# A 512-byte-piece fill of the last output rows on ScalarE's DMA queue at the start, and one store left whole, in an L1 row normalisation

## The chip, the cores and the metric

The kernel runs on one core of one Trainium2 chip. The metric is the device time of one execution in microseconds (us). Three executions of the kernel before took 317.07, 317.03 and 316.71 us, a median of 317.03 us.

## The reference, cut to what matters

The input is 32 x 512 x 1024 numbers in float32, that is 16384 rows of 1024. Each row is divided by the sum of its absolute values:

```python
sums = np.sum(np.abs(x), axis=-1, keepdims=True)
return (x / (sums + 1e-8)).astype(np.float32)
```

67.11 MB are read and 67.11 MB are written.

## The kernel before, in words

The 16384 rows are cut into eleven pieces. A piece covers all 128 partitions of the on-chip memory, with 12 rows of 4 KB per partition (6.29 MB); the last piece (number 10, `last` in the code) has 8 rows per partition (4.19 MB). Pieces 0, 1 and 10 come out of the first 4096 rows, where each partition has 32 consecutive rows: rows 0 to 11 are piece 0, rows 12 to 23 are piece 1, rows 24 to 31 are piece 10. Pieces 2 to 9 follow one after the other. There are four buffers of one piece each.

Every piece goes through the same four steps.

- **Load** (L86): one DMA issued by SyncE (SP). The argument `max_dma_last_dim` sets how large a contiguous run one DMA piece may carry: 48 KB (the whole run of a partition) for loads 0 and 1, 24 KB for the others. A DMA over 128 partitions is spread over the 16 DMA engines, 8 partitions on each, so each engine gets 8 pieces of 48 KB for load 0, 8 of 48 KB for load 1, and 16 of 24 KB for each load from 2 to 9 (load 10: 16 of 16 KB).
- **Sum** (L47): VectorE (DVE) sums the absolute values of each row, then adds epsilon (L54) and takes the reciprocal (L56).
- **Scale**: most rows are multiplied on VectorE in one instruction (L58); for pieces 0, 1, 2, 9 and 10 the table `split` gives some rows to ScalarE (ACT, L68) and some to single-row instructions on VectorE (L65).
- **Store** (L91): DMAs issued by ScalarE's queue, with 24 KB runs for pieces 0 to 8 and the whole run for pieces 9 and 10. Stores 7 and 8 (`last - 3` and `last - 2`) are issued as two DMAs of half a piece each, all others as one.

The order of the program is written out by hand (`manual_schedule`): loads 0 to 3 first, then for each piece its compute, its store, and the load of the piece four further on, which takes over the buffer and so waits until that store has landed. Loads are on SP's queue, stores on ScalarE's queue; both queues are served by the same 16 DMA engines. The waits between engines and DMAs are put in by the framework. It gives every DMA one of eight completion semaphores in turn, and a DMA also waits for the one that held its semaphore before.

Of the kernel before, what the change touches and what calls it, by code (L numbers as in the profile page):

```python
# [1 line left out]

# [4 lines left out]

FP32 = mybir.dt.float32
EPS = 1e-8


@with_exitstack
def kernel(
    ctx: ExitStack,
    tc: tile.TileContext,
    x: bass.AP,
    out: bass.AP,
):
    nc = tc.nc
    P = nc.NUM_PARTITIONS  # L20

    x_flat = x.flatten_outer_dims()
    out_flat = out.flatten_outer_dims()
    n, d = x_flat.shape

    R = 12
    BUFS = 4
    HEAD = 32
    per_partition = n // P
    assert n % P == 0 and (per_partition - HEAD) % R == 0  # L30
    rows = [R] * ((per_partition - HEAD) // R + 2) + [HEAD - 2 * R]

    def piece(flat, i):
        head = flat[: P * HEAD, :].rearrange("(p r) d -> p r d", p=P)
        if i < 2:
            return head[:, R * i : R * (i + 1), :]
        if i == len(rows) - 1:
            return head[:, 2 * R :, :]
        a = P * (HEAD + R * (i - 2))
        return flat[a : a + P * R, :].rearrange("(p r) d -> p r d", p=P)  # L40

    sbuf = ctx.enter_context(tc.tile_pool(name="sbuf", bufs=BUFS))
    stats = ctx.enter_context(tc.tile_pool(name="stats", bufs=len(rows)))

    def normalize(x_tile, k, kv, kt):
        s = stats.tile([P, R], FP32)
        nc.vector.tensor_reduce(  # L47
            out=s[:, :k],
            in_=x_tile[:, :k, :],
            axis=mybir.AxisListType.X,  # L50
            op=mybir.AluOpType.add,
            apply_absolute_value=True,
        )
        nc.vector.tensor_scalar_add(out=s[:, :k], in0=s[:, :k], scalar1=EPS)  # L54
        inv = stats.tile([P, R], FP32)
        nc.vector.reciprocal(out=inv[:, :k], in_=s[:, :k])  # L56
        if kv:
            nc.vector.tensor_mul(  # L58
                out=x_tile[:, :kv, :],
                in0=x_tile[:, :kv, :],  # L60
                in1=inv[:, :kv].unsqueeze(2).to_broadcast([P, kv, d]),
            )
        for r in range(kv, kv + kt):
            row = x_tile[:, r, :]
            nc.vector.tensor_scalar_mul(out=row, in0=row, scalar1=inv[:, r : r + 1])  # L65
        for r in range(kv + kt, k):
            row = x_tile[:, r, :]
            nc.scalar.activation(  # L68
                out=row,
                in_=row,  # L70
                func=mybir.ActivationFunctionType.Copy,
                scale=inv[:, r : r + 1],
            )

    last = len(rows) - 1
    split = {0: (3, 4), 1: (0, 3), 2: (0, 3), last - 1: (0, 2), last: (5, 3)}

    tiles = {}

    HALF, WHOLE = 24576, 49152

    def load(i):
        x_tile = tiles[i] = sbuf.tile([P, R, d], FP32, name="x_tile")
        nc.sync.dma_start(out=x_tile[:, : rows[i], :], in_=piece(x_flat, i), max_dma_last_dim=WHOLE if i < 2 else HALF)  # L86

    def store(i):
        parts = [(0, R // 2), (R // 2, R)] if i in (last - 3, last - 2) else [(0, rows[i])]
        for a, b in parts:  # L90
            nc.scalar.dma_start(  # L91
                out=piece(out_flat, i)[:, a:b, :],
                in_=tiles[i][:, a:b, :],
                max_dma_last_dim=WHOLE if i >= last - 1 else HALF,
            )

    def compute(i):
        k = rows[i]
        kt, ks = split.get(i, (0, 0))
        normalize(tiles[i], k, k - kt - ks, kt)  # L100

    with tc.manual_schedule():
        for i in range(BUFS):
            load(i)
        for i in range(len(rows)):
            compute(i)
            store(i)
            if i + BUFS < len(rows):
                load(i + BUFS)


# [1 line left out]
_INS = ['x']  # L113
_OUTS = [((32, 512, 1024), 'float32')]


# [23 lines left out]
```

## Time and profile before

| quantity | value |
|---|---|
| median of three executions | 317.03 us |
| the profiled execution | 316.79 us |
| span of its instructions in the profile | 315.2 us |
| VectorE busy | 261.1 us (83%) |
| ScalarE busy | 17.4 us (6%) |
| read from and written to the off-chip memory (HBM) | 67.11 MB each, 426 GB/s over the span |
| first load issued; first sum starts | 0.73 us; 17.72 us |
| store 0 issued | 38.75 us |
| last store issued | 292.51 us |

The profile is of one execution. Its span runs from the first to the last recorded instruction; the device time of the same execution is 1.6 us longer, because of what lies around it. Views of the trace give, for any stretch of the span, the busy time of each engine, the busy share of the 16 DMA engines, the bytes they moved and how many DMA packets each queue had. A packet is booked in the stretch in which it starts, so the rate of a short stretch jumps, and only stretches of many packets can be compared closely. In these views q1 is SP's queue (the loads) and q10 is ScalarE's queue (the stores). The trace also holds every packet's own start, duration, size and queue.

### The profile page before, as it was taken

The numbers are of one execution on the slowest core, as the hardware profiler recorded it, in microseconds if no ns is written. First come the engines' busy times: TensorE is split into PE (matmuls) and PEld (weight loads), VectorE is DVE, ScalarE is ACT, GpSimd is POOL, SyncE is SP. The second block draws the span as 40 slices with busy tenths as digits, with TensorE's granted clock in tenths as the row PEclk, the third lists the DMA queues.
The fourth block names the chain that finished last, engine by engine and source line by source line (L and its number), as shares of the span: only waits on it lengthen the run. The fifth ranks groups of instructions, "written<-read, shape, count | busy, mean of one in ns | idle before, by whom it ended". The sixth has DMA issues, their size and how long they took to land.

```text
span 315.2 us, 169 instructions
## 1 busy us (share of the span) xinstructions
DVE 261.1 (83%) x51; ACT 17.4 (6%) x16; POOL 0.2 (0%) x4
## 2 busy tenths in 40 slices
DVE  0079999999999999979996997999699969999100
ACT  0010403004000000000000000000000000203000
POOL 0000000000000000000000000000000000000000
DMA  7999999999999999999999999999999999999997
GB/s 299 499 399 409 440 399 418 430 449 418 430 449 418 430 449 424 424 449 427 421 449 427 421 449 434 415 449 434 415 449 434 415 433 449 416 433 499 399 403 329
DMA packets 5504, 134.22 MB, mean 426 GB/s; under 512 B 384, under 2 KB 384, under 8 KB 384
## 3 DMA queue, kind: packets, MB, share of 16 engines
q1 hardware_dynamic: 2736, 67.11, 49.9%
q10 hardware_dynamic: 2768, 67.11, 49.4%
HBM read 67.11 MB, written 67.11 MB: 426 GB/s over the span
## 4 chain that ended last, share of the span: by engine, by line
DVE 41%; DMA 33%; another core or an unknown queue 18%; SPq 0%; issue 0%; DVEq 0%
DVE s L47 23%; DMA x_tile<-in_x_dram 17%; DVE x_tile L58 15%; DMA out_dram<-x_tile 15%; DVE x_tile L65 2%; DVE inv L56 0%; DVE s L54 0%; SPq L86 0%; DVEq L135 0%
## 5 line engine op out<-in xcount | busy, mean ns | idle before, releaser
L47 DVE TENSOR_REDUCE s<-x_tile 128x12 f32<-128x12288 f32 (+1 forms) x11 | 138.2, 12561 | 30.0 <-DMA x_tile<-in_x_dram 30.0
L58 DVE TENSOR_TENSOR x_tile<-x_tile,inv 128x12288 f32<-128x12288 f32 (+3 forms) x10 | 113.6, 11358 | 0.5
L68 ACT ACTIVATE x_tile<-x_tile,inv 128x1024 f32<-128x1024 f32 x15 | 16.1, 1138 | 257.1 <-DVE inv L56 257.1
L65 DVE TENSOR_SCALAR x_tile<-x_tile,inv 128x1024 f32<-128x1024 f32 x8 | 5.5, 748 | 0.0
L56 DVE RECIPROCAL inv<-s 128x12 f32<-128x12 f32 (+1 forms) x11 | 2.5, 226 | 0.4
L68 ACT ACT_TABLE_LOAD x1 | 1.3, 1283 | 17.8 <-DMA x_tile<-in_x_dram 17.8
L54 DVE TENSOR_SCALAR s<-s 128x12 f32<-128x12 f32 (+1 forms) x11 | 1.9, 173 | 0.4
L124 POOL MEMSET const-uint8-127<- 128x1 uint8 x1 | 0.1, 102 | 0.0
L124 POOL MEMSET const-bfloat16-1.0<- 128x1 bf16 x1 | 0.1, 101 | 0.0
L124 POOL MEMSET const-float32-0.0<- 128x1 f32 x1 | 0.1, 98 | 0.2 <-issue 0.2
L124 POOL MEMSET const-float32-1.0<- 128x1 f32 x1 | 0.1, 98 | 0.0
## 6 DMA issues: line engine op xcount, KB each, us to landing
x_tile<-in_x_dram SPq DMA_DIRECT2D x10, 6144.0 KB, 37.6
out_dram<-x_tile ACTq DMA_DIRECT2D x8, 6144.0 KB, 47.2
out_dram<-x_tile ACTq DMA_DIRECT2D x4, 3072.0 KB, 36.5
x_tile<-in_x_dram SPq DMA_DIRECT2D x1, 4096.0 KB, 32.0
out_dram<-x_tile ACTq DMA_DIRECT2D x1, 4096.0 KB, 21.7
```

Of the source, the lines that this page charges most:

```text
L47: nc.vector.tensor_reduce(out=s[:, :k], in_=x_tile[:, :k, :], axis=mybir.AxisListType.X, op=mybir.AluOpType.add, apply_absolute_value=True,)
L54: nc.vector.tensor_scalar_add(out=s[:, :k], in0=s[:, :k], scalar1=EPS)
L56: nc.vector.reciprocal(out=inv[:, :k], in_=s[:, :k])
L58: nc.vector.tensor_mul(out=x_tile[:, :kv, :], in0=x_tile[:, :kv, :], in1=inv[:, :kv].unsqueeze(2).to_broadcast([P, kv, d]),)
L65: nc.vector.tensor_scalar_mul(out=row, in0=row, scalar1=inv[:, r : r + 1])
L68: nc.scalar.activation(out=row, in_=row, func=mybir.ActivationFunctionType.Copy, scale=inv[:, r : r + 1],)
L124: nc = _bacc.Bacc("TRN2", target_bir_lowering=False, num_devices=1)
```

## The change

A second pool with one small tile is added. After load 0 is issued, a new function `fill` sets this tile (128 x 128 float32) to zero on VectorE, and ScalarE's queue issues one DMA from it. The DMA writes the first 384 numbers of the first row of piece 10 in every partition, as 3 chunks of 512 bytes: 3 chunks x 8 partitions is 24 pieces of 512 bytes on each DMA engine, 196,608 bytes in all. Store 10, the last one, writes the final values over these bytes. Besides, store 7 (`last - 3`) is no longer split: it is issued as one DMA with 24 KB runs, like stores 0 to 6. Store 8 stays split.

```diff
     sbuf = ctx.enter_context(tc.tile_pool(name="sbuf", bufs=BUFS))
+    once = ctx.enter_context(tc.tile_pool(name="once", bufs=1))
     stats = ctx.enter_context(tc.tile_pool(name="stats", bufs=len(rows)))
...
-        parts = [(0, R // 2), (R // 2, R)] if i in (last - 3, last - 2) else [(0, rows[i])]
+        parts = [(0, R // 2), (R // 2, R)] if i == last - 2 else [(0, rows[i])]
...
+    CHUNKS, WIDTH = 3, 128
+
+    def fill():
+        zeros = once.tile([P, WIDTH], FP32, name="zeros")
+        nc.vector.memset(zeros, 0.0)
+        nc.scalar.dma_start(
+            out=piece(out_flat, last)[:, 0, : CHUNKS * WIDTH].rearrange("p (c w) -> p c w", c=CHUNKS),
+            in_=zeros.unsqueeze(1).to_broadcast([P, CHUNKS, WIDTH]),
+            max_dma_last_dim=4 * WIDTH,
+        )
+
     with tc.manual_schedule():
-        for i in range(BUFS):
+        load(0)
+        fill()
+        for i in range(1, BUFS):
             load(i)
```

## The prediction

> **What bounds the kernel now.** I read the page first.
>
> ```profile
> span 315.2 us, 169 instructions
> ...
> DVE 261.1 (83%) x51; ACT 17.4 (6%) x16; POOL 0.2 (0%) x4
> ...
> DMA  7999999999999999999999999999999999999997
> ...
> DMA packets 5504, 134.22 MB, mean 426 GB/s; under 512 B 384, under 2 KB 384, under 8 KB 384
> ...
> q1 hardware_dynamic: 2736, 67.11, 49.9%
> q10 hardware_dynamic: 2768, 67.11, 49.4%
> ```
>
> No compute engine fills the span, but the DMA row is full from the second slice to the next to last, and the packets of both queues together fill 99.3% of sixteen engines' span. The waits say the same from VectorE's side: it has 30 us of idle time, all of it for loads.
>
> ```profile
> DVE s L47 <- DMA x_tile<-in_x_dram: 30.0, 6, 17.7
> ```
>
> So bytes bound it, and the question is at which moments the DMA engines are not moving them. I cut the span into stretches of 27.25 us, thirty 24 KB pieces each (columns: stretch, length, busy time of DVE, ACT and POOL, clock, DMA share, GB/s).
>
> ```profile
> 13.42:40.67 27.25, 22.84 (x8) 5.55 (x5) 0.00 (x0) 1.00 1.00 431
> 40.67:67.92 27.25, 27.15 (x5) 3.23 (x3) 0.00 (x0) 1.00 1.00 420
> 67.92:95.17 27.25, 27.15 (x5) 3.23 (x3) 0.00 (x0) 1.00 1.00 433
> ...
> 204.17:231.42 27.25, 24.50 (x5) 0.00 (x0) 0.00 (x0) 1.00 1.00 433
> ```
>
> Loads alone (first line) run at 431, loads and stores together at 433. One stretch is short: 420 against 433 is 27.25 x 13 / 433 = 0.82 us lost. It holds the moment when ScalarE's queue gets its first work. Store 0 is issued at 38.75, and the view of the DMA queues from 40.48 to 43.17 shows
>
> ```profile
> DMA packets 33, 0.81 MB, mean 301 GB/s; under 512 B 0, under 2 KB 0, under 8 KB 0
> ...
> q1 hardware_dynamic: 33, 0.81, 100.3%
> ```
>
> that is only load packets, "busy" all the time, but at 301: 2.69 x (1 - 301/433) = 0.82 us again. In the single packet records a 24 KB packet takes 0.912 us wherever it stands, except two per engine here; together these are 0.82 us too long (mean of 16 engines, 0.77 to 0.86 in the six I took apart). Then the first store packet goes at 43.17, 4.4 us after the issue. After this the two queues alternate, one piece of each, to the end, with no gap; all other packets after 43 us are 0.02 us too long in sum. The first packet of load 0 is also too long, 2.62 against 1.815 us, by 0.80 on the mean. So an idle queue that gets work seems to cost each engine about 0.8 us: once at the start for SP's queue, once at 41 us for ScalarE's. I read the second as a fixed cost of waking a queue; that it is this and not, say, the first write to HBM is an inference.
>
> The budget closes: first packet at 1.73, all packets at their usual rate 310.07, the two losses 0.80 + 0.82, the small rest 0.02: 313.44, and the engines' last packets end between 313.33 and 313.85. Then 1.3 us to the span's end, and 1.6 us more to the execution's 316.79. The median of 317.03 is 0.24 above this; I add my sum to the median.
>
> **The change part by part.**
>
> *The fill's bytes.* DMA engines have no slack, so this is paid in full. The usual distance from one packet to the next is 0.607 us for 16 KB, 0.908 for 24 KB, 1.210 for 32 KB, 1.812 for 48 KB, 0.0055 for the 4-byte completion packets. That is 36.8 ps per byte and about 5 ns per packet, so 512 bytes cost 19 + 5 = 24 ns and 24 of them 0.57 us. The trace has no packet between 4 bytes and 16 KB. From below, the bytes alone are 0.45 us; from above, a small write that holds its engine for twice my value gives 1.14. I take 0.57, as 4-byte packets, also small, cost only their 5 ns.
>
> *The stall at 41 us.* If ScalarE's queue never runs dry between the start and store 0, waking it happens at about 2 us. ScalarE waits for VectorE's memset (nearest rows: 0.17 us for a 128x12 operation, 0.75 for 128x1024), so it issues at about 1.1, against 0.73 for load 0. Load 0's first packets start 1.0 us after their issue and lose their 0.80 until about 2.6, so the wake of ScalarE's queue, from about 2.1 on, falls on engines of which most still wait for their first bytes. Between hidden (gain 0.82) and not hidden (gain 0) I take hidden, because both queues' losses have the same size and look like one latency, and two latencies can run together.
>
> *Does the queue stay awake?* One piece of each queue goes in turn, and even the 4-byte completion packets take a turn of their own, so 24 small pieces last as long as 24 load pieces: 8 of load 0, 8 of load 1, 8 of load 2. In the records the 8th piece of load 2 ends at 38.8; with 0.57 us of fill ahead, 39.4. Store 0's issue comes 8 x 24 ns = 0.19 later with load 0's landing, at 38.94, and its first packets can start 1.0 later, at 39.9. So the queue is dry for 0.5 us, or not at all if its pieces go one or two load pieces late (0.9 us each), as store 0's first did. This is close; I take the second.
>
> [...] The records of this trace show turns of one piece, but none of 512 bytes.
>
> [...]
>
> *The memset and the early issue.* VectorE is idle until 17.72 and ScalarE until 17.77, so both are hidden. SP's loads 1 to 3 are issued after the fill in the program's text but on another engine, with no wait on it. Eight small pieces make load 0 land 0.19 us later, and VectorE's first sum with it; VectorE's work ends at 292.5 while stores keep the DMA engines busy to 313.8, so it has some 11 us of cover (store 9 ends at 304.2 and store 10 is issued at 292.5). Without that cover it would cost these 0.19 us.
>
> *New waits.* Load 5 takes the fill's semaphore and waits for it, but is issued past 100 us, some 60 us after the fill has landed. Store 10 must follow the fill too, at 292. Nothing queues behind either.
>
> *Store 7 whole.* Removed: one DMA issue of ScalarE's queue (0.34 to 0.48 us on an engine that is 94% idle) and one 4-byte packet per engine, 0.0055 us, which pays for the fill's own. Moved: its first half no longer lands at 260.1 but with the second, at 272.9. No load follows into this buffer, so nobody waits. Store 9's semaphore is then one last held by load 8, long done. Below and above: nothing.
>
> Sum: -0.82 + 0.57 = **-0.25 us**: 316.54 for the profiled execution, 316.8 on the median.
>
> **The rivals.**
>
> *A. The wake is hidden at the start* (as above): -0.25, or up to +0.2 if half of it shows. For it: the engines stand still at the start anyway. Against: ScalarE's queue wakes some 0.4 us after SP's, so part may stick out. 316.8 (316.5 to 317.3).
>
> *B. The stall moves but does not shrink*, or the change does not do what it says and it stays at 41 us (several small pieces go in one turn, or the cost belongs to something that only a large store meets): +0.57, 317.6; 318.2 with small pieces at 48 ns. For it: nothing in the trace shows two wakes overlapping.
>
> *C. It is paid twice* (this one ends slower): the queue wakes unhidden at 2 us, runs dry before store 0's descriptors come, and wakes again at 41 us: 0.82 + 0.57 = +1.39, 318.4. It decides when the last small piece goes over 0.5 us before 39.9, which is where my reckoning without lag puts it, and when an empty queue loses its state at once.
>
> *D. Stall gone and small pieces nearly free*, because they are written while the engine waits for a load's reads: their 5 ns each are 0.12, so -0.82 + 0.12 = -0.70, 316.3. Against: loads and stores in turn run at 433, no faster than loads alone at 431, so nothing is covered in that way.
>
> **How the numbers follow.** A 0.48, B 0.30, C 0.14, D 0.08. The bound of 0.2%, 0.63 us, is about what a measurement of this kernel can tell from no change. A lies within it. B lies within it at 24 ns a piece and outside from 27 ns; I split it in halves. C is slower; D is just faster. Faster 0.08, same 0.63, slower 0.29. The range: from 316.2 (D) to 318.2 (B with its upper cost), which leaves out C and a little of the others, some 0.18 in all. A's own range is 316.5 to 317.3.
>
> **What would show it.** In the changed profile q10 has 24 x 16 = 384 more packets, "under 2 KB" but not "under 512 B", and 16 fewer and 16 more 4-byte ones. If A holds, the stretch after 40 us is at 433 and q10 packets appear in it at once; the first packets of q1 take about as long as before. B shows the start (306 GB/s between 1.70 and 4.27 us now) slow for longer, or 420 still in that stretch; C both. If small pieces cost more than 24 ns, loads 0 and 1 land later than by 0.2 and 0.4 us. I am wrong altogether if another stretch, above all one after 250 us, falls below 433, or if VectorE's last work moves past 304.

## The result, and the profile after

The changed kernel takes 317.62 us against 316.85 for the kernel before (medians of 12 executions each): a ratio of 1.0027, 95% interval 1.0018 to 1.0035, or +0.77 us (0.57 to 1.11). It is slower, by 0.27%; the forecast was 316.8, faster.

Its page, with the counts of DMA packets, the two queues, and the last line of the list of DMA issues (KB, then us from issue to landing):

```profile
span 315.8 us, 171 instructions
...
DMA packets 5888, 134.42 MB, mean 426 GB/s; under 512 B 384, under 2 KB 768, under 8 KB 768
...
q1 hardware_dynamic: 2736, 67.11, 49.8%
q10 hardware_dynamic: 3152, 67.31, 49.5%
...
out_dram<-zeros ACTq DMA_DIRECT2D x1, 192.0 KB, 39.0
```

The 384 small packets are there (768 under 2 KB, still 384 under 512 bytes), on q10. The fill landed 39.0 us after its issue. The single packet records give the kernel's last packet the end 314.31 (313.85 before). The timeline gives the moments that the prediction reckoned with:

```profile
1.02 0.45 ACTq L108 DMA_DIRECT2D out_dram<-zeros  x1
17.93 12.95 DVE L48 TENSOR_REDUCE s<-x_tile 128x12 f32<-128x12288 f32 x1 [16.94 <-DMA x_tile<-in_x_dram]
...
38.96 0.38 ACTq L92 DMA_DIRECT2D out_dram<-x_tile  x1
```

The first sum starts 0.21 us later than before (0.19 was expected) and store 0 is issued at 38.96 (38.94). So the early part went as reckoned. Now the stretches of 27.25 us (length, busy times, clock, DMA share, GB/s):

```profile
13.42:40.67 27.25, 22.63 (x8) 5.55 (x5) 0.00 (x0) 1.00 1.02 437
40.67:67.92 27.25, 27.15 (x5) 3.23 (x3) 0.00 (x0) 1.00 1.00 418
67.92:95.17 27.25, 27.15 (x5) 3.23 (x3) 0.00 (x0) 1.00 1.00 433
```

The short stretch is still there, 418 where it was 420. The view of the DMA queues from 40.90 to 43.50, which holds two whole turns of every engine:

```profile
DMA packets 32, 0.79 MB, mean 302 GB/s; under 512 B 0, under 2 KB 0, under 8 KB 0
...
q1 hardware_dynamic: 32, 0.79, 102.3%
```

32 load packets of 24 KB, none of q10, at 302 GB/s: the same picture as before, 0.5 us later (the first packet of store 0 starts at 43.65, before at 43.17). By the single packet records the long packets here add up to 0.84 us per engine (0.82 before). At the start, load 0's first packets are too long by 0.70 (0.80 before), but they also start 0.10 later on the mean, so these two cancel. The small pieces are 0.0235 us apart from what follows them, 0.564 us for 24. The engines' last packets end 0.55 us later on the mean of the 16 (313.54 to 314.09): that is the fill's bytes to within 0.02. The span grew by more, 0.68 us; the rest lies behind the last packet and is taken up in the account of the sum below.

So the time came from the fill itself, and the stall that it was to move stayed. The question for the chip is what that stall belongs to. Two theories at first: **Dry**, which the prediction rests on: it is the cost of waking a queue that has run dry; in the changed kernel the last small piece went at 38.3 to 38.8 and the fill's completion packets at 39.3 to 39.7, while store 0, issued at 38.96, had its first piece at 43.65. And **Large store**: it comes with the first large store pieces among loads, whatever the queue did before.

### The profile page after: what moved, and what is told of

Read it like the earlier page. It is cut to its first block, busy times and chain, and to the rows that moved or that the text cites. A ratio compares the mean times of both kernels' runs of the same rounds, so it can differ in the third digit from the quotient of the medians.

```text
span 315.8 us, 171 instructions
## 1 busy us (share of the span) xinstructions
DVE 261.4 (83%) x52; ACT 17.4 (6%) x16; POOL 0.2 (0%) x4
## 4 chain that ended last, share of the span: by engine, by line
DVE 41%; DMA 33%; another core or an unknown queue 18%; SPq 0%; issue 0%; DVEq 0%
DVE s L48 23%; DMA x_tile<-in_x_dram 18%; DVE x_tile L59 15%; DMA out_dram<-x_tile 15%; DVE x_tile L66 1%; DVE inv L57 0%; DVE s L55 0%; SPq L87 0%; DVEq L149 0%
```

## Experiments

In what follows "the loss" is the sum of what load packets take beyond their usual time, per engine, the mean of 16, read from the packet records of the one profiled execution of each kernel.

**fill32: the queue fed until store 0 comes.**

```diff
-    CHUNKS, WIDTH = 3, 128
+    CHUNKS, WIDTH = 4, 128
```

> Four chunks instead of three: 32 pieces of 512 bytes per DMA engine. In the changed kernel the last of the 24 small pieces ended at about 39.4 us and store 0's descriptors came some 0.5 us later. Theory Dry (an engine loses about 0.82 us when ScalarE's queue gets work after it has run dry): the queue is still fed when store 0 comes, the two long load packets at 41 us vanish, and the time is the kernel before - 0.82 + 32 x 0.0235 = -0.07 us, about 316.8. Theory Large store (the loss belongs to the first large piece that the queue carries, whatever went before): the two long packets are still there just before store 0's first piece, and the time is before + 0.75 = 317.6, a little above the changed kernel.

Measured: 317.99 against 316.78 us, ratio 1.0037 (1.0025 to 1.0050), above what either theory had. Store 0 was issued at 39.13, and small pieces went out until 46.8 to 47.2, one after each load piece. Two stretches of the DMA queues, each with three load pieces and three small ones per engine; first 41.5 to 44.3 us:

```profile
DMA packets 96, 1.20 MB, mean 430 GB/s; under 512 B 0, under 2 KB 48, under 8 KB 48
...
q10 hardware_dynamic: 48, 0.02, 2.9%
```

then 44.3 to 47.5 us:

```profile
DMA packets 96, 1.20 MB, mean 376 GB/s; under 512 B 0, under 2 KB 48, under 8 KB 48
...
q10 hardware_dynamic: 48, 0.02, 2.5%
```

The same packets, but 376 for 430 GB/s. The queue is awake, as q10's 48 packets show, and load packets are long all the same (0.49 us by the records). They stand 5 us after store 0's issue, and just ahead of its first piece at 47.8. So this loss stands ahead of the first store piece in the order of packets; it does not follow the issue and does not need a dry queue. Dry falls. Odd in this profile: another 0.46 us of slightly long load packets between 12 and 36 us. The kernel after and the next one don't have them; the two amounts together are about the usual loss.

**fill32_64b: the same with 64-byte pieces.**

```diff
-    CHUNKS, WIDTH = 3, 128
+    CHUNKS, WIDTH = 4, 16
```

> 32 pieces of 64 bytes per DMA engine. By the spacing of packets (36.8 ps per byte and 4.7 ns per packet) a piece costs 7 ns and all of them 0.23 us. Theory Dry: before - 0.82 + 0.23 = -0.59 us, about 316.25, faster than both kernels. Theory Large store: before + 0.23, about 317.1. If pieces under 512 bytes cost as much as those of 512, 0.5 us is to be added to either.

Measured: 317.27 against 316.78, ratio 1.0015 (1.0006 to 1.0024): +0.49 us, interval 0.19 to 0.76. The windows:

```profile
13.42:40.67 27.25, 22.86 (x8) 5.55 (x5) 0.00 (x0) 1.00 1.00 429
40.67:67.92 27.25, 27.15 (x5) 3.23 (x3) 0.00 (x0) 1.00 1.00 420
```

The loss is 0.72 us although small pieces went out until 45.4 to 45.9 and the first store piece followed at 46.9. The 7 ns for a 64-byte piece stay an estimate from the spacing of other packets; by the times, 32 of them came with +0.49 us where fill32's 32 of 512 bytes came with +1.21, so pieces under 512 bytes are not dearer here. Large store (+0.23) is within the interval, Dry (-0.59) is not.

**no_fill: the other half of the change alone.**

```diff
         load(0)
-        fill()
         for i in range(1, BUFS):
```

> Only the second half of the change: store 7 left whole, no zeros written. Both theories: no difference from the kernel before beyond 0.1 us, as nobody waits for the first half of store 7. A rival in which leaving store 7 whole is what costs the 0.77 us has 317.6 here.

Measured: 316.79 against 316.78, ratio 1.0002 (0.9993 to 1.0011). Leaving store 7 whole costs nothing; the loss before store 0 is 0.82. All of the change's time comes with the fill (its memset, its DMA and its bytes).

**late8: a dry queue woken among flowing loads.**

```diff
-    CHUNKS, WIDTH = 3, 128
+    CHUNKS, WIDTH = 1, 128
...
-        nc.vector.memset(zeros, 0.0)
+        for _ in range(36):
+            nc.vector.memset(zeros, 0.0)
```

> One chunk (8 pieces of 512 bytes per DMA engine), issued only after 36 memsets on VectorE, so at some 7 to 12 us, while load packets flow; the queue then runs dry long before store 0. Theory Dry with a cost for every waking: 0.8 us of long load packets some 2.5 us after the issue of the fill and again 0.84 at 41 us, together before + 0.8 + 0.19 = 317.85. Theory Large store: nothing at the fill, 0.82 at 41 us, before + 0.19 = 317.05.

The fill was issued at 10.06 us; its small pieces went from 13.6 us on. The view of the DMA queues from 9.0 to 14.5 us, then from 14.5 to 20.0, three turns each:

```profile
DMA packets 54, 2.36 MB, mean 430 GB/s; under 512 B 0, under 2 KB 6, under 8 KB 6
```

```profile
DMA packets 128, 2.39 MB, mean 435 GB/s; under 512 B 16, under 2 KB 80, under 8 KB 80
```

430 and 435: waking ScalarE's queue among flowing loads costs nothing that can be seen (0.002 us in the records). Before store 0 the loss is 0.92. So this waking, with small pieces, had no price. Yet the kernel took 317.63 against 316.78 us (1.0026, 1.0016 to 1.0037), not the 317.05 of Large store; by the time alone it is nearer to Dry's 317.85. Its page has a line that the kernel before hasn't:

```profile
q14 instruction: 1, 0.01, 0.0%
```

One 8 KB packet of instructions, at 129.04 us. By the records it takes 0.31 us on one of the 16 engines and the load packet behind it is 0.53 us too long. One engine's last packet then ends at 314.63, the others' at 314.00 or before, and the kernel ends with its slowest engine; that it is the same engine is inferred. 0.19 + 0.6 = 0.8, beside 0.85 measured. The kernels before and after have such packets only ahead of the span and behind it (at 315.78 and 316.16 us). I take the added memsets for its cause, which no run here isolates: late8_4k and late8_12k below, with 7 and 2 added, have such a packet in their spans, early8_12k with none added has not.

**late8_4k and late8_12k: larger zero pieces.** 8 pieces per engine as in late8, of 4 KB and of 12 KB, with 8 and 3 longer memsets in place of 36. For 4 KB:

```diff
-    CHUNKS, WIDTH = 3, 128
+    CHUNKS, WIDTH = 1, 1024
...
-        nc.vector.memset(zeros, 0.0)
+        for _ in range(8):
+            nc.vector.memset(zeros, 0.0)
```

For 12 KB:

```diff
-    CHUNKS, WIDTH = 3, 128
+    CHUNKS, WIDTH = 3, 1024
...
-        zeros = once.tile([P, WIDTH], FP32, name="zeros")
-        nc.vector.memset(zeros, 0.0)
+        zeros = once.tile([P, CHUNKS, WIDTH], FP32, name="zeros")
+        for _ in range(3):
+            nc.vector.memset(zeros, 0.0)
...
-            out=piece(out_flat, last)[:, 0, : CHUNKS * WIDTH].rearrange("p (c w) -> p c w", c=CHUNKS),
-            in_=zeros.unsqueeze(1).to_broadcast([P, CHUNKS, WIDTH]),
-            max_dma_last_dim=4 * WIDTH,
+            out=piece(out_flat, last)[:, :CHUNKS, :],
+            in_=zeros,
+            max_dma_last_dim=4 * CHUNKS * WIDTH,
```

> 8 zero pieces of 4 KB per DMA engine, issued at some 9 us among flowing loads; their bytes are 8 x 0.156 = 1.25 us. late8 showed that pieces of 512 bytes make no long load packet there. Theory Volume (the loss grows with the store data that the engine has under way): a few tenths of a us of long load packets near the first 4 KB pieces. Theory Large piece (only a piece of tens of KB, or the real store, brings it): none there, 0.8 us before store 0 as always.

> 8 zero pieces of 12 KB per DMA engine, issued at some 10 us among flowing loads and long done before store 0; their bytes are 8 x 0.457 = 3.65 us. Theory Volume: 0.4 to 0.8 us of long load packets near the first zero pieces. If the loss is paid once for the whole program, store 0 has then only the rest of the 0.8 us before it; if it is paid each time that large stores set in among loads, store 0 has 0.8 again. A theory in which it belongs to store 0 itself (its issue, its rows) has nothing at the zeros and 0.8 at store 0.

One execution each: 318.68 and 320.79 us against 316.88; both also have an instruction packet inside the span, so the losses say more than the times. With 4 KB the loss at the fill is 0.13, before store 0 it is 0.85. With 12 KB it is 0.52 at the fill and only 0.23 before store 0. The view of the DMA queues of late8_12k from 9.0 to 14.5 us (before its first zero piece; 0.09 of the loss stands there), then from 12.5 to 17.1, with two load pieces and the first zero piece of every engine:

```profile
DMA packets 48, 2.36 MB, mean 429 GB/s; under 512 B 0, under 2 KB 0, under 8 KB 0
```

```profile
DMA packets 48, 1.77 MB, mean 385 GB/s; under 512 B 0, under 2 KB 0, under 8 KB 0
...
q1 hardware_dynamic: 32, 1.57, 90.3%
q10 hardware_dynamic: 16, 0.20, 10.0%
```

The rate falls where the first 12 KB pieces come in; after 17.1 us no load packet is long until store 0. So the loss does not belong to store 0 alone, and what was paid at the fill was largely not paid again.

**early8_12k: the same, earlier.** As late8_12k with one memset instead of three:

```diff
-        for _ in range(3):
-            nc.vector.memset(zeros, 0.0)
+        nc.vector.memset(zeros, 0.0)
```

> The 8 zero pieces of 12 KB as in late8_12k but after one memset instead of three, at some 4 us, so that the store queue is dry for about 20 us before store 0 instead of 13. If the loss is paid once for the program up to the largest volume so far, the zeros take 0.4 to 0.55 us and store 0 only the rest, 0.2 to 0.3, as in late8_12k. If the smaller loss at store 0 there came from stores still under way or from chance, store 0 takes 0.8 here. Time before + 3.65 either way, within 0.6.

Measured: one execution, 320.53 against 316.87. The zeros' pieces went from 7.9 to 23 us, the first store piece about 23 us later. Loss 0.47 at the fill and 0.15 before store 0. The view of the DMA queues from 12.4 to 17.0 us (the third and fourth zero piece of every engine), then from 17.0 to 19.7 (the fifth, and the load piece behind it):

```profile
DMA packets 64, 1.97 MB, mean 427 GB/s; under 512 B 0, under 2 KB 0, under 8 KB 0
```

```profile
DMA packets 32, 0.98 MB, mean 364 GB/s; under 512 B 0, under 2 KB 0, under 8 KB 0
...
q1 hardware_dynamic: 16, 0.79, 83.0%
q10 hardware_dynamic: 16, 0.20, 17.0%
```

So the small rest in late8_12k was not chance: the larger part of the loss is paid once, even with the store queue dry in between. But the place speaks against a simple count of store data. By the records 0.45 us of late8_12k's loss and 0.43 of this kernel's stand in one and the same load packet, the eighth and last of load 0, just ahead of load 0's completion packet: there behind the first zero piece, here behind the fifth. Volume, and the end of a load with large stores under way, are both left as readings.

**one_8k: one large piece beside the start.** 16 partitions, one 8 KB piece per engine, after one memset.

```diff
-    CHUNKS, WIDTH = 3, 128
+    CHUNKS, WIDTH = 2, 1024
...
-        zeros = once.tile([P, WIDTH], FP32, name="zeros")
-        nc.vector.memset(zeros, 0.0)
+        zeros = once.tile([P, CHUNKS, WIDTH], FP32, name="zeros")
+        nc.vector.memset(zeros[:16], 0.0)
...
-            out=piece(out_flat, last)[:, 0, : CHUNKS * WIDTH].rearrange("p (c w) -> p c w", c=CHUNKS),
-            in_=zeros.unsqueeze(1).to_broadcast([P, CHUNKS, WIDTH]),
-            max_dma_last_dim=4 * WIDTH,
+            out=piece(out_flat, last)[:16, :CHUNKS, :],
+            in_=zeros[:16],
+            max_dma_last_dim=4 * CHUNKS * WIDTH,
```

> One zero piece of 8 KB per DMA engine (16 partitions, 2 rows each), issued after one memset at 2 to 4 us; its bytes are 0.306 us. If the loss is paid once for the program and can be hidden beside load 0's first latency, the long packets before store 0 are gone or shorter and the time is up to 0.5 us under the kernel before, 316.3. If it is paid each time, the time is before + 0.3 = 317.1 with 0.8 us of long packets before store 0.

Measured: 317.48 against 316.88, ratio 1.0022 (1.0012 to 1.0031). No loss at the piece (7.9 us), 1.07 before store 0. This single 8 KB piece took none of the loss over. The engines' last packets end 0.53 later on the mean, near the sum of its bytes (0.31) and a larger loss (+0.25).

**s0_on_sp: store 0 in the loads' own queue.**

```diff
-            nc.scalar.dma_start(
+            (nc.sync if i == 0 else nc.scalar).dma_start(
                 out=piece(out_flat, i)[:, a:b, :],
...
-        fill()
```

> No zeros; store 0 goes on SP's queue, behind load 3, so that its pieces come in the same queue as the loads and ScalarE's queue gets its first work with store 1 at 62 us. A theory in which a second queue that sets in costs 0.8 us: nothing at store 0's first pieces near 60 us, long load or store packets 2 to 3 us after store 1's issue. A theory in which stores among loads cost it, whichever queue carries them: the long packets stand where store 0's first pieces enter, near 60 us, whichever queue has them. The total is not compared, since load 4 now waits in SP's queue behind store 0.

Measured: one execution, 316.68 against 316.88. The view of the DMA queues from 56.7 to 58.5 us, then from 58.5 to 60.9 (two load pieces per engine each, the last of load 3, with store 0 behind them in the same queue), then from 63.7 to 67.3, where ScalarE's queue gets its first work ever:

```profile
DMA packets 32, 0.79 MB, mean 437 GB/s; under 512 B 0, under 2 KB 0, under 8 KB 0
```

```profile
DMA packets 32, 0.79 MB, mean 328 GB/s; under 512 B 0, under 2 KB 0, under 8 KB 0
...
q1 hardware_dynamic: 32, 0.79, 101.0%
```

```profile
DMA packets 64, 1.57 MB, mean 437 GB/s; under 512 B 0, under 2 KB 0, under 8 KB 0
...
q1 hardware_dynamic: 48, 1.18, 76.0%
q10 hardware_dynamic: 16, 0.39, 25.3%
```

437, 328, 437. The two load packets ahead of store 0 are long (0.60 us by the records) with a single queue at work, and the first pieces of the second queue cost nothing. So neither a second queue nor its first work is needed for the loss. Nor need stores come among loads: load 4 waits here for store 0's buffer, so behind load 3 only stores ran. Store 1's first piece still came 3.9 us after its issue, so that delay, which I had put beside the stall, is another thing; what it is made up of was not shown.

**pieces48k and pieces12k: the size of a piece.** From no_fill, with the 24 KB runs made 48 or 12 KB.

```diff
-    HALF, WHOLE = 24576, 49152
+    HALF, WHOLE = 49152, 49152
```

> No zeros; every load and every store but store 8 in runs of 48 KB per partition (store 8's halves stay at 24 KB). 128 packets fewer per DMA engine at 4.7 to 4.9 ns of spacing each: -0.6 us. If the loss at store 0 is a fixed 0.82 us, the time is the kernel before - 0.6 = 316.2. If the loss grows with the size of a store piece (0.13 us after eight of 4 KB, 0.52 after eight of 12 KB, 0.82 with 24 KB so far), it is 1.2 to 1.6 us here, and the time is 316.6 to 317.0.

> No zeros; loads 2 to 9 and stores 0 to 8 in runs of 12 KB. 272 packets more per DMA engine, +1.3 us. If the loss at store 0 is fixed, its long load packets sum to 0.82 us; if it grows with the size of a store piece, to 0.4 to 0.55 us. Time 318.2 or 317.9.

pieces48k: 317.39 against 316.87, ratio 1.0017 (1.0006 to 1.0027), slower although it has 137 packets fewer per engine (load 10 goes in larger runs too, and one completion packet falls away with store 7 whole). The loss is 1.08 at store 0 and another 0.36 in small amounts at later places; and the engines drift apart: their last packets end between 312.98 and 314.50 (313.33 to 313.85 before), and the slowest counts; the mean, 313.55, is as before. pieces12k: one execution, 318.21 against 316.87, +1.34 for 287 packets more, 4.7 ns each; loss 0.87. So with 12 KB and 24 KB pieces the loss is the same, and only at 48 KB a little larger: "grows with the size of a piece" falls for real stores. What made the 12 KB zeros take over 0.5 us and the 4 KB zeros 0.13 is not settled by these runs.

The losses together, us per engine:

| kernel | near the fill | before store 0 | sum |
|---|---|---|---|
| before | - | 0.82 | 0.82 |
| no_fill | - | 0.82 | 0.82 |
| after (24 x 512 B) | 0.00 | 0.84 | 0.84 |
| fill32 (32 x 512 B) | 0.46 | 0.49 | 0.95 |
| fill32_64b (32 x 64 B) | 0.00 | 0.72 | 0.72 |
| late8 (8 x 512 B) | 0.00 | 0.92 | 0.92 |
| late8_4k | 0.13 | 0.85 | 0.98 |
| late8_12k | 0.52 | 0.23 | 0.75 |
| early8_12k | 0.47 | 0.15 | 0.62 |
| one_8k | 0.00 | 1.07 | 1.07 |
| s0_on_sp | - | 0.60 (0.06 more later) | 0.66 |
| pieces12k | - | 0.87 | 0.87 |
| pieces48k | - | 1.08 (0.36 more later) | 1.44 |

Each row is one execution. Among the kernels that store as the kernel before does and paid little or nothing earlier, the loss before store 0 lies between 0.72 and 1.07, so differences of 0.2 or 0.3 between rows may be scatter; the 0.23 and 0.15 of the 12 KB kernels lie outside it.

## Why the prediction was wrong, point by point

- **What bounds the kernel**: right. The DMA engines have no slack: 0.564 us of added pieces moved their last packets by 0.55.
- **The fill's bytes**, 0.57 us at 24 ns a piece from the spacing of packets 30 to 90 times as large: right, 0.564 us measured. The upper bound of twice that was an assumption that no run shows, and D, which had these pieces at 0.12, is out.
- **Turns**: that several small pieces go in one turn, which B allowed, did not happen. Each 512-byte piece took one turn, as the 24 KB pieces do; in fill32, 48 load packets and 48 small ones went between 41.5 and 44.3 us.
- **The stall at 41 us**: this is the step that failed. It said that an idle queue that gets work costs each engine 0.8 us, and that this waking could be hidden beside the load's own start. The text called the reading an inference, and then gave its alternative only a clause within B, with no chance of its own. So the term -0.82 of the sum came out as +0.02: in the changed kernel the loss was 0.84 at the same place. late8 shows a waking that cost nothing, fill32 and fill32_64b that a queue kept awake does not prevent the loss, s0_on_sp that it comes without any second queue. In every kernel without large zeros it stands at the first store pieces behind loads (in fill32 half of it); what in them brings it stays open. That load 0's first packets were long by a like amount (0.80 and 0.82) was taken for one mechanism; the numbers show no tie between the two: load 0's stays at 0.6 to 0.8 in all thirteen profiles, while the other goes from 0.15 to 1.08.
- **Does the queue stay awake**: the reckoning of 39.4 without lag was nearly right (the queue's last packet went at 39.3 to 39.7, the last small piece at 38.3 to 38.8), and the lag of one or two load pieces that I chose was not: the first small piece did go two load pieces late, but the completion packets of loads 0 and 1 took turns as well, and small pieces used these. It did not matter, as fill32 shows.
- **Early issue, new waits, store 7 whole**: right at nothing; no_fill gives 1.0002 for the last. The memset was hidden at the start too, but see the next point.
- **Sum**: +0.57 - 0.82 became +0.57 + 0.02. The measured +0.77 (0.57 to 1.11) holds this at its lower end; the profiles give +0.55 for the mean engine, +0.46 for the one that ends last and +0.68 for the span. The other 0.21 us lies behind the last packet, where the sum had 1.3 us with nothing to change it: 1.31 before, 1.52 after. VectorE's last DRAIN, one of the program's closing instructions, starts 0.75 us behind the last packet before and 1.16 after. The tail is 1.51 to 1.53 in all five kernels with a fill and no instruction packet inside the span, 1.31 to 1.36 in the five without a fill, 1.14 to 1.26 in the three with such a packet inside; so the times of fill32, fill32_64b and one_8k hold the same 0.2. That the fill's memset in VectorE's program brings it is a guess; no run has the fill without a memset.
- **The rivals**: B was what happened, in its second form ("the cost belongs to something that only a large store meets"), at its 317.6. C's condition (a dry queue) was met and the price of its first waking, 0.82 at the start, was not paid: load 0's first packets were long by 0.70, less than before.

What stays open: why the first large stores cost an engine 0.6 to 1.1 us, and whether it is their volume or their place that counts; why fill32 has part of it between 12 and 36 us; and whether a real early store could pay it where it is free. No version here is shown to beat the kernel before: one_8k and fill32_64b, which tried to pay the loss elsewhere or cheaply, are slower by 0.22% and 0.15%.

## What to carry to other kernels

Here the DMA engines were full from end to end (99.3% of their span before) and the fill's bytes were paid in full: 0.564 us of pieces moved the last packets by 0.55. The cost of the small pieces could be read well from the spacing of large ones (0.57 us reckoned, 0.564 measured). A stall found beside an event has several neighbours (a queue's first work, an issue, a change from loads to mixed traffic): before building a remedy on one of them, move each alone. Where the gain hangs on such a reading, the reading that fails deserves its own rival with its own chance.

## What was not expected of the hardware

- In these kernels each DMA engine lost 0.6 to 1.1 us when the first large stores came in behind loads, mostly in the last load packets ahead of the first store piece, whichever queue carried it. Eight 12 KB pieces took 0.5 us of it in advance, eight 512-byte pieces none; it did not come back in full after the store queue had been dry for 13 and 23 us (0.23 and 0.15 then).
- Instructions seem to be read by the same DMA engines: one 8 KB packet inside late8's span took 0.31 us, one load packet just behind it was 0.53 us too long, and one engine ended 0.6 us after the rest.
- Small pieces were cheap between large ones: 23.5 ns of spacing for 512 bytes (the kernel after), 155 ns for 4 KB (late8_4k). For 64 bytes there is the estimate of 7 ns (36.8 ps a byte and 4.7 ns a packet) and fill32_64b's time, +0.49 us with 32 of them.
- Runs of 48 KB saved 137 packets per engine and still lost 0.5 us: the mean engine ended as before, but the 16 ends lay 1.5 us apart (0.5 before).
